# One transpose of the identity in front of each run of 256-column products that follows 512-column ones

## The chip, the cores and the metric

The kernel runs on one core of one Trainium2 chip. The metric is the device time of one execution in microseconds (us); the profile comes from one profiled execution, whose own time is given beside its span. TensorE is called PE below, its weight loads PEld; VectorE is DVE, ScalarE is ACT, GpSimd is POOL, SyncE is SP.

## The reference, cut to what matters

Two transformer blocks run one after the other on 256 positions of width 2048, all in float32.

```python
def first_block(x, mem, ...):
    mem_h = rms_norm(mem, mem_norm_g)
    x = x + hybrid_mixer(rms_norm(x, mix_norm_g), w_in, ...)          # pooling and a gated delta rule
    x = x + memory_cross_attention(rms_norm(x, xa_norm_g), mem_h, w_xq, w_xkv, w_xo)
    x = x + conv_glu_ffn(rms_norm(x, ffn_norm_g), w_gate, w_up, conv_w, conv_b, w_down)   # 2048 -> 5632 -> 2048
    return rms_norm(x, final_norm_g)

def second_block(x, c, ...):
    ...                                                                # six vectors from silu(c) @ w_ada
    x = x + gate_m * rms_norm_2(o, post_norm_mix)                      # o: two attentions and w_o
    h = modulate(rms_norm_2(x, pre_norm_ffn), shift_f, scale_f)
    f = jnp.square(jax.nn.relu(h @ w_up)) @ w_down                     # 2048 -> 8192 -> 2048
    x = x + gate_f * rms_norm_2(f, post_norm_ffn)
    return x
```

Nearly all the arithmetic is in the large products with a weight matrix: w_in, w_xkv, w_xq, w_xo, w_mix_out, w_gate, w_up, w_down and their namesakes of the second block.

## The kernel before, in words

A float32 product is made of three products of tiles of the type `F32R`: every weight tile w is split into a high part `wh` and the rest `wl`, every activation tile into `h` and `lo`, and h·wh, h·wl and lo·wh are summed in PSUM. The weights are walked in *groups* of 512 output columns (class `Group`, a few of 256), and a group in *units* of 512 KB: a DMA on SP's queue brings a unit into `w32` (`load_to`, seven units ahead), ACT writes `wh` (L216), DVE subtracts and writes `wl` (L218), and PE uses both.

There are two routines for a group. `lin_a` gives the result with the positions on the partitions: the activation is the stationary operand and 512 columns of the weight stream past it (L300, L301, L302; 256 columns in the few narrow groups). `lin_b` gives the result transposed: a block of 128 weight columns is the stationary operand and the 256 positions stream past it (L318, L319, L320). These are called *long* and *short* products below. A short group has 16 blocks of rows, each with four blocks of columns and three products, 192 products in all; a long group over 16 blocks of rows has 96, over 8 blocks 48, four such groups in a row 192.

`lin_b` makes the pooled, convolved, key and query columns, and the gate and up columns of both feed-forward parts; `lin_a` makes what must have the positions on the partitions: z, the values, and all products that go back into the residual. So the two kinds alternate: in the first feed-forward part two slabs of gate and up (768 short products), then one w_down slab (192 long ones); in the second, 384 short and 192 long ones, eight times.

The program is written in order; there is no scheduler. After each unit `pump` advances the tasks that run beside the products: attention, the delta rule, evacuations, and `ada`, which multiplies silu(c) into w_ada on DVE and turns each finished sum with four transposes on PE (L1179). Such small PE work therefore stands between the products of two units, in line on PE's queue. A transpose is a matmul with the 128x128 identity `ident` of the constant tile `cst` as the streamed operand, float32, 128 columns.

Accumulators are PSUM tiles `acc0` to `acc3`, two for each group; small work uses four other banks, `m0` to `m3`.

Of the kernel before, what the change touches and what calls it, by code (L numbers as in the profile page):

```python
# [15 lines left out]
P = 128  # L16
# [65 lines left out]
class Group:  # L82
    def __init__(self, w, segs, k0=0, nkb=KB):
        self.w, self.segs, self.k0, self.nkb = w, segs, k0, nkb
        self.n = sum(b - a for a, b in segs)
        self.calm = False
        step = 1024 // self.n
        self.units = [(self, kb, step) for kb in range(0, nkb, step)]


class Prog:
# [3 lines left out]
    def __init__(self, ctx, tc, i, o, dbg=None):  # L95
        self.tc, self.nc, self.i, self.o, self.dbg = tc, tc.nc, i, o, dbg
        self.pool = ctx.enter_context(tc.tile_pool(name="s", bufs=1))
        self.wpool = ctx.enter_context(tc.tile_pool(name="w", bufs=3))
        self.w32pool = ctx.enter_context(tc.tile_pool(name="w32", bufs=4))
        self.psum = ctx.enter_context(tc.tile_pool(name="ps", bufs=1, space=bass.MemoryType.PSUM))  # L100
        ctx.enter_context(tc.manual_schedule())
        self.seq = 0
        self.tasks = []
        self.evacs = []
        self.free_banks = ["m0", "m1", "m2", "m3"]
        self.acc_next = 0
        self.named = {}
        self.small = {}
        self.blocked = False
        self.relief = set()  # L110
        self.busy = set()
        self.rr = None
# [174 lines left out]
    def lin_a(self, g, xh, xl, evac, ready=None, eager=False):  # L287
        mm = self.nc.tensor.matmul
        n = g.n
        accs = [a[:, :n] for a in self.group_start()]  # L290
        for _, kb0, nk in g.units:
            self.check_ready(ready, kb0)
            wh, wl = self.take(g)
            for k in range(nk):
                kb = kb0 + k
                for tb in range(2):
                    ps = accs[tb]
                    h = xh(kb)[:, tb * P:(tb + 1) * P]
                    lo = xl(kb)[:, tb * P:(tb + 1) * P]
                    mm(ps, h, wh[:, k, :], start=kb == 0, stop=False)  # L300
                    mm(ps, h, wl[:, k, :], start=False, stop=False)  # L301
                    mm(ps, lo, wh[:, k, :], start=False, stop=kb == g.nkb - 1)  # L302
            self.pump()
        return self.finish_group(evac(accs), eager)

    def lin_b(self, g, xh, xl, evac, ready=None):
        mm = self.nc.tensor.matmul
        accs = self.group_start()
        for _, kb0, nk in g.units:
            self.check_ready(ready, kb0)  # L310
            wh, wl = self.take(g)
            for k in range(nk):
                kb = kb0 + k
                h, lo = xh(kb), xl(kb)
                for b in range(4):
                    ps = accs[b // 2][:, (b % 2) * T:(b % 2 + 1) * T]
                    wb, wb2 = wh[:, k, b * P:(b + 1) * P], wl[:, k, b * P:(b + 1) * P]
                    mm(ps, wb, h, start=kb == 0 and b % 2 == 0, stop=False, skip_group_check=True)  # L318
                    mm(ps, wb, lo, start=False, stop=False, skip_group_check=True)  # L319
                    mm(ps, wb2, h, start=False, stop=kb == g.nkb - 1, skip_group_check=True)  # L320
            self.pump()
        return self.finish_group(evac([a.rearrange("p (b t) -> p b t", b=2) for a in accs]))
# [1672 lines left out]
```

## Time and profile before

| | us |
|---|---|
| median of 3 runs | 2728.62 (2727.25 to 2729.43) |
| profiled execution, its own time | 2727.51 |
| its span | 2725.7 |
| PE busy | 2681.1 (98%) |
| PE weight loads busy | 2480.4 (91%) |
| DVE busy | 1854.2 (68%) |
| ACT busy | 1302.8 (48%) |
| POOL busy | 255.5 (9%) |
| mean granted clock of PE | 0.995 of full speed |

The profiled execution's time is 1.1 us below the median, and its span 1.8 us below its time. Matmuls are pipelined, so PE's busy times overlap one another: a short product "lasts" 280 ns in the rows, but the next one starts after some 115 ns. The pace, which is what a stretch costs, is therefore read as the length of a stretch divided by the products in it, and the count of weight loads (PEld) is the better count: one for each product, and hardly any that reach over the edge of the stretch.

### The profile page before, as it was taken

To read this page: it belongs to the slowest core of one execution; us is meant where nothing else is said; L and a number is where in the kernel's file an instruction comes from. 1 tells how busy PE (TensorE), PEld (TensorE's weight loads), DVE (VectorE), ACT (ScalarE), POOL (GpSimd) and SP (SyncE) were. 2 spreads that over 40 slices of the span, in tenths; PEclk is the share of its full clock that TensorE was granted. 3 is DMA by queue.
4 is the path that set the end of the run, shared out by engine and by line. 5 is a ranking of instruction groups with operands and counts; after the bars stand their busy time and mean duration, and the time that the engine had idled before them with its cause. 6 is when DMAs were issued, how large, how long until landed. Compare 5 with 4: busy or idle time off the path is not lost.

```text
span 2725.7 us, 45971 instructions
## 1 busy us (share of the span) xinstructions
PE 2681.1 (98%) x18466; PEld 2480.4 (91%) x18466; DVE 1854.2 (68%) x2331; ACT 1302.8 (48%) x1924; POOL 255.5 (9%) x229
## 2 busy tenths in 40 slices
PE   8999999999999999999999999999989999999998
PEld 8999998889989999999999888997889988999897
DVE  6665745677687778787778586677675556655555
ACT  6544533554445455354544564444554444444443
POOL 0230211000000021010100001001011000000020
PEclk9999999999999999999999999999999999999999
DMA  8644644688788888888887656544557767766654
GB/s 290 201 126 130 191 121 140 216 295 272 228 270 266 272 259 272 275 265 283 271 270 263 210 164 178 147 146 128 173 181 235 236 218 241 232 190 193 189 186 151
DMA packets 293126, 584.33 MB, mean 214 GB/s; under 512 B 21920, under 2 KB 36384, under 8 KB 292912
## 3 DMA queue, kind: packets, MB, share of 16 engines
q1 hardware_dynamic: 288528, 568.41, 65.6%
q0 software_dynamic: 3664, 11.67, 1.4%
q8 instruction: 145, 2.38, 0.4%
q10 hardware_dynamic: 720, 1.31, 0.1%
q14 instruction: 69, 0.57, 0.1%
HBM read 579.21 MB, written 2.10 MB: 213 GB/s over the span
## 4 chain that ended last, share of the span: by engine, by line
PE 93%; DVE 3%; ACT 2%; issue 1%; POOL 0%; DMA 0%; SPq 0%; DVEq 0%; POOLq 0%; ACTq 0%
PE acc L318 16%; PE acc L319 16%; PE acc L320 16%; PE acc L300 12%; PE acc L301 12%; PE acc L302 12%; DVE wl L218 1%; ACT wh L216 1%; PE m L998 1%; PE m L1051 1%; PE m L1058 1%; PE m L1148 1%; PE m L1117 1%; PE m L1001 0%; PE m L1179 0%
## 5 line engine op out<-in xcount | busy, mean ns | idle before, releaser
L218 DVE TENSOR_TENSOR wl<-w,wh 128x1024 fp32r<-128x1024 f32 x880 | 1097.1, 1249 | 805.2 <-ACT wh L216 802.8
L216 ACT ACTIVATE wh<-w 128x1024 fp32r<-128x1024 f32 x880 | 927.9, 1058 | 1121.4 <-PE acc L319 614.3
L318 PE MATMUL acc<-A,wh 128*128 128x256 f32 x3968 | 1124.1, 283 | 9.3 <-ACT A L406 7.8
L319 PE MATMUL acc<-A,wh 128*128 128x256 f32 x3968 | 1112.6, 280 | 0.7 <-DVE A L1430 0.7
L320 PE MATMUL acc<-A,wl 128*128 128x256 f32 x3968 | 1112.0, 280 | 0.8 <-DVE wl L218 0.8
L318 PEld LDWEIGHTS acc<-A,wh 128*128 128x128 f32 x3968 | 750.6, 189 | 11.4 <-ACT A L406 7.8
L320 PEld LDWEIGHTS acc<-A,wl 128*128 128x128 f32 x3968 | 756.7, 191 | 1.0 <-DVE wl L218 1.0
L319 PEld LDWEIGHTS acc<-A,wh 128*128 128x128 f32 x3968 | 749.2, 189 | 2.6 <-DVE A L1430 1.2
L300 PE MATMUL acc<-wh,A 128*128 128x512 f32 (+1 forms) x1584 | 616.0, 389 | 0.3 <-DVE r L1264 0.3
L301 PE MATMUL acc<-wl,A 128*128 128x512 f32 (+1 forms) x1584 | 608.3, 384 | 1.2 <-DVE wl L218 1.2
L302 PE MATMUL acc<-wh,A 128*128 128x512 f32 (+1 forms) x1584 | 607.8, 384 | 0.0
L301 PEld LDWEIGHTS acc<-wl,A 128*128 128x128 f32 x1584 | 298.1, 188 | 60.5 <-DVE wl L218 4.5
L302 PEld LDWEIGHTS acc<-wh,A 128*128 128x128 f32 x1584 | 297.8, 188 | 59.3
L300 PEld LDWEIGHTS acc<-wh,A 128*128 128x128 f32 x1584 | 298.0, 188 | 57.2 <-issue 0.9
L1200 DVE SCALAR_TENSOR_TENSOR r<-r,c_silu_c,r 128x1024 f32<-128x1024 f32 x128 | 170.1, 1329 | 0.0
L1200 DVE SCALAR_TENSOR_TENSOR s<-s,c_silu_c,s 128x512 f32<-128x512 f32 x128 | 95.8, 748 | 15.7 <-DMA s<-w_ada 14.4
L1886 POOL TENSOR_TENSOR s<-s 128x512 f32<-128x512 f32 x32 | 50.9, 1592 | 581.5 <-ACT s L1885 581.5
L1255 POOL TENSOR_TENSOR r<-r,rr 128x1024 f32<-128x1024 f32 x11 | 27.9, 2536 | 570.3 <-ACT r L1254 527.5
L1730 ACT ACTIVATE s<-s,c_am 128x128 f32<-128x128 f32 (+1 forms) x48 | 21.5, 448 | 92.0 <-DVE c_am L1728 92.0
L1618 POOL TENSOR_TENSOR r<-r,s 128x512 f32<-128x512 f32 x15 | 25.6, 1704 | 263.7 <-DVE s L1615 263.7
L1251 DVE SCALAR_TENSOR_TENSOR r<-r,prm,r 128x254 f32<-128x254 f32 x88 | 42.4, 481 | 1.6
L378 ACT ACTIVATE dd<-X 128x512 bf16<-128x512 f32 (+1 forms) x42 | 25.5, 606 | 21.4 <-DVE X L441 15.6
(375 smaller groups left out, 1611.8 us busy)
## 6 DMA issues: line engine op xcount, KB each, us to landing
w<-w_up SPq DMA_DIRECT2D x216, 512.0 KB, 3.8
w<-w_down SPq DMA_DIRECT2D x216, 512.0 KB, 3.9
w<-w_in SPq DMA_DIRECT2D x152, 512.0 KB, 3.7
r<-w_ada SPq DMA_DIRECT2D x128, 512.0 KB, 5.2
w<-w_gate SPq DMA_DIRECT2D x88, 512.0 KB, 4.3
w<-w_xkv SPq DMA_DIRECT2D x64, 512.0 KB, 3.9
s<-w_ada SPq DMA_DIRECT2D x128, 256.0 KB, 5.1
w<-w_mix_out SPq DMA_DIRECT2D x32, 512.0 KB, 3.7
```

The source lines that it names most:

```text
L216: nc.scalar.activation(hi[:, :m], src[:, :m], AF.Copy)
L218: eng.tensor_tensor(lo[:, :m], src[:, :m], hi[:, :m].bitcast(F32), op=OP.subtract)
L300: mm(ps, h, wh[:, k, :], start=kb == 0, stop=False)
L301: mm(ps, h, wl[:, k, :], start=False, stop=False)
L302: mm(ps, lo, wh[:, k, :], start=False, stop=kb == g.nkb - 1)
L318: mm(ps, wb, h, start=kb == 0 and b % 2 == 0, stop=False, skip_group_check=True)
L319: mm(ps, wb, lo, start=False, stop=False, skip_group_check=True)
L320: mm(ps, wb2, h, start=False, stop=kb == g.nkb - 1, skip_group_check=True)
L1200: nc.vector.scalar_tensor_tensor(acc, tiles.pop(n), self.silu_c[:, kb:kb + 1], acc, op0=OP.mult, op1=OP.add)
L1251: nc.vector.scalar_tensor_tensor(cv[:, b, s:], st[:, b, :T - s], w[k], cv[:, b, s:], op0=OP.mult, op1=OP.add)
L1255: nc.gpsimd.tensor_tensor(cv, cv, self.rr[:, None, :].to_broadcast([P, 4, T]), op=OP.mult)
L1886: nc.gpsimd.tensor_tensor(y, y, y, op=OP.mult)
```

## The change

Every run of short products that comes after long ones gets one transpose of the identity by itself in front of its first product. It writes the first 128 columns of the group's first accumulator, which the group's first product then starts anew (`start`), so no result depends on it. A flag `narrow` says whether long products have run since: `lin_a` clears it, `settle` sets it.

```diff
@@ class Prog, __init__
+        self.narrow = True
@@ lin_a
         accs = [a[:, :n] for a in self.group_start()]
+        self.narrow = False
         for _, kb0, nk in g.units:
@@
+    def settle(self, ps):
+
+        self.narrow = True
+        for r in range(1):
+            self.nc.tensor.transpose(ps[:, r * P:(r + 1) * P], self.c("ident"), self.c("ident"))
+
     def lin_b(self, g, xh, xl, evac, ready=None):
         mm = self.nc.tensor.matmul
         accs = self.group_start()
         for _, kb0, nk in g.units:
             self.check_ready(ready, kb0)
             wh, wl = self.take(g)
+            if not self.narrow:
+                self.settle(accs[0])
             for k in range(nk):
```

The program gains 17 transposes on PE and nothing on any other engine. Line numbers behind it grow by ten. On PE's queue, where the third down slab of the first feed-forward part ends and the gate columns of the next slabs begin, stood before (`acc_737` is the last accumulator of the down group, `acc_744` the first of the gate group):

```order
L301 MATMUL acc_737_11542<-wl_11566,A_629_8934 128x512
L302 MATMUL acc_737_11542<-wh_11565,A_630_8935 128x512
L318 MATMUL acc_744_11629<-A_540_7873,wh_11584 128x256 [waits Activation_49]
L319 MATMUL acc_744_11629<-A_542_7875,wh_11584 128x256
L320 MATMUL acc_744_11629<-A_540_7873,wl_11585 128x256 [waits DVE_49]
```

and stands now, with the transpose as L312:

```order
L303 MATMUL acc_737_11546<-wl_11570,A_629_8937 128x512
L304 MATMUL acc_737_11546<-wh_11569,A_630_8938 128x512
L312 MATMUL acc_744_11633<-cst 128x128
L328 MATMUL acc_744_11633<-A_540_7875,wh_11588 128x256 [waits Activation_49]
L329 MATMUL acc_744_11633<-A_542_7877,wh_11588 128x256
L330 MATMUL acc_744_11633<-A_540_7875,wl_11589 128x256 [waits DVE_49]
```

The transpose stands between the last long product and the first short one and waits for nothing; what the short products wait for is as it was. Thirteen of the 17 stand so, straight behind long products. The other four have small PE work in front of them. One is the first run of the first feed-forward part, where four transposes of `ada` stand there already; now:

```order
L1189 MATMUL m_588_8315<-cst,s_546_7899 128x128 [waits DMASW0_49,DVE_49,PE_49]
L1189 MATMUL m_588_8315<-cst,s_546_7899 128x128 x3
L312 MATMUL acc_591_8322<-cst 128x128
L328 MATMUL acc_591_8322<-A_540_7875,wh_8271 128x256 [waits Activation_49]
L329 MATMUL acc_591_8322<-A_542_7877,wh_8271 128x256
```

Here the new transpose is the fifth in a row.

## Rows read from the trace of the kernel before

**Rows 1.** The page: engines' busy time, and the chain that ended last.

```profile
PE 2681.1 (98%) x18466; PEld 2480.4 (91%) x18466; DVE 1854.2 (68%) x2331; ACT 1302.8 (48%) x1924; POOL 255.5 (9%) x229
...
PE 93%; DVE 3%; ACT 2%; issue 1%; POOL 0%; DMA 0%; SPq 0%; DVEq 0%; POOLq 0%; ACTq 0%
PE acc L318 16%; PE acc L319 16%; PE acc L320 16%; PE acc L300 12%; PE acc L301 12%; PE acc L302 12%; DVE wl L218 1%; ACT wh L216 1%; PE m L998 1%; PE m L1051 1%; PE m L1058 1%; PE m L1148 1%; PE m L1117 1%; PE m L1001 0%; PE m L1179 0%
```

**Rows 2.** The page's groups: line, shape, count, busy us, mean ns, idle before.

```profile
L318 PE MATMUL acc<-A,wh 128*128 128x256 f32 x3968 | 1124.1, 283 | 9.3 <-ACT A L406 7.8
...
L300 PE MATMUL acc<-wh,A 128*128 128x512 f32 (+1 forms) x1584 | 616.0, 389 | 0.3 <-DVE r L1264 0.3
```

**Rows 3.** Windows: length, busy (xcount) by engine, clock, DMA; short stretches behind long products.

```profile
612.87:641.13 28.26, 28.26 (x241) 28.26 (x240) 22.04 (x25) 11.76 (x12) 0.00 (x0) 1.00 0.90 308
986.36:1076.82 90.46, 90.46 (x770) 90.45 (x768) 72.66 (x71) 42.02 (x46) 9.41 (x6) 1.00 0.84 272
...
2579.09:2624.32 45.23, 45.23 (x386) 45.23 (x385) 22.09 (x21) 18.98 (x20) 3.19 (x2) 1.00 0.63 188
sum 463.58, PE 463.58 PEld 463.55 DVE 307.61 ACT 199.88 POOL 29.26; mean PE 42.14 PEld 42.14 DVE 27.96 ACT 18.17 POOL 2.66
```

**Rows 4.** Windows: short stretches behind groups of transposes.

```profile
1192.71:1211.85 19.14, 19.14 (x172) 19.14 (x170) 15.19 (x18) 11.43 (x20) 2.41 (x2) 1.00 0.74 233
1295.66:1344.72 49.06, 49.06 (x435) 49.06 (x434) 37.37 (x39) 25.24 (x34) 4.90 (x3) 1.00 0.80 262
1400.27:1476.53 76.26, 76.26 (x676) 76.26 (x674) 61.79 (x64) 38.06 (x48) 5.90 (x2) 1.00 0.83 272
2411.35:2446.81 35.46, 35.46 (x316) 35.46 (x314) 17.13 (x15) 16.91 (x25) 3.20 (x2) 1.00 0.63 193
870.00:960.00 90.00, 90.00 (x766) 90.00 (x766) 71.62 (x74) 42.30 (x47) 4.84 (x2) 1.00 0.85 280
2017.00:2088.00 71.00, 71.00 (x605) 71.00 (x604) 42.52 (x42) 34.02 (x40) 9.54 (x6) 1.00 0.76 246
```

**Rows 5.** Timeline of PE (start us, us): a short run straight behind long products.

```profile
986.14 0.39 PE L302 MATMUL acc<-wh,A 128*128 128x512 f32 x1
986.36 0.28 PE L318 MATMUL acc<-A,wh 128*128 128x256 f32 x1
986.48 0.28 PE L319 MATMUL acc<-A,wh 128*128 128x256 f32 x1
```

**Rows 6.** Timeline of PE: four transposes between short products.

```profile
1292.01 0.28 PE L320 MATMUL acc<-A,wl 128*128 128x256 f32 x1
1292.13 0.60 PE L1179 MATMUL m<-cst,r 128*128 128x128 f32 x4
1292.49 0.37 PE L318 MATMUL acc<-A,wh 128*128 128x256 f32 x1
1292.69 0.28 PE L319 MATMUL acc<-A,wh 128*128 128x256 f32 x1
```

**Rows 7.** Timeline of PE: four transposes between long and short products.

```profile
823.87 0.39 PE L302 MATMUL acc<-wh,A 128*128 128x512 f32 x1
824.10 0.60 PE L1179 MATMUL m<-cst,s 128*128 128x128 f32 x4
824.45 0.36 PE L318 MATMUL acc<-A,wh 128*128 128x256 f32 x1
824.65 0.28 PE L319 MATMUL acc<-A,wh 128*128 128x256 f32 x1
```

**Rows 8.** Timeline of PE: three transposes behind long products, further on.

```profile
1791.00 0.49 PE L1744 MATMUL m<-cst,s 128*128 128x128 f32 x3
1791.24 0.36 PE L318 MATMUL acc<-A,wh 128*128 128x256 f32 x1
```

**Rows 9.** Timeline of PE: four transposes between short products, in front of 870.

```profile
863.61 0.60 PE L1179 MATMUL m<-cst,s 128*128 128x128 f32 x4
863.97 0.36 PE L318 MATMUL acc<-A,wh 128*128 128x256 f32 x1
```

## The prediction

> **What bounds the kernel now.** I read the page's busy line first, then the chain that ended last, then the groups of PE, then windows cut exactly to single runs of products, and the timeline at their edges. PE is busy 98% of the span and holds 93% of the chain [rows 1]. Within it the short products (L318 to L320) hold 48% of the chain and the long ones (L300 to L302) 36% [rows 1]; in front of L318 PE sat idle for only 9.3 us of the whole span, 7.8 of them in one wait for ACT [rows 2]. So no other engine's edge matters here: the time is the number of products times the pace at which PE takes them.
>
> The pace of short products is the point. A window cut to one run gives it as length over weight loads. Straight behind long products the run of 768 from 986.36 takes 90.45 to 90.46 us, which is 117.8 ns for one; the eleven such stretches that are long enough to read take 463.58 us together [rows 3], at the same pace 3936 products. The same instructions on tiles of the same shape, at the same granted clock of 1.00, go faster in the four stretches of rows 4 that begin behind a group of transposes: with two loads at the edge taken off each, 168, 432, 672 and 312 products take 19.14, 49.06, 76.26 and 35.46 us, which is 113.6 ns with the slow first product (0.20 us instead of 0.12 [rows 6, 5]) and 113.4 without it. Neither pace drifts within a run: 840 products keep the slower one through 870 to 960, and 672 the faster one through 1400 to 1476 [rows 4]. Two paces, 4.4 ns apart, which a run takes on at its start and keeps: I read that as two ways in which weight loads and products can interlock, between which only an interruption moves PE. The rows don't show what the interlock is.
>
> Behind that sentence stands the Trainium skill, TensorE: Matmul & The Clock Gate, section Back-to-back issue gap: it gives the gap of warm products as a function of their columns alone, N/2.4 + 2.5, an estimate of 109.2 ns for 256 columns. The trace disagrees, with 117.8 and 113.4 ns for one shape, and it decides.
>
> **The change part by part.** It removes nothing and moves nothing but PE's rows by one. It adds 17 transposes. Thirteen stand straight behind long products, four behind small PE work.
>
> What one costs. Rows 7 show four transposes in that very place: from the start of the last long product (823.87) to that of the second short one (824.65) is 0.78 us, against 0.34 us with nothing between (986.14 to 986.48 [rows 5]). That is 0.44 us for four and 0.11 us for one. Rows 6 give the same: 1292.01 to 1292.69 is 0.68 us where two gaps of 0.12 stood, so 0.44 for four. Seventeen cost 17 x 0.11 = 1.9 us, all of it on PE and so on the chain. From below the cost is not under zero, as nothing is taken out for it; from above 0.24 us, if a lone one pays what rows 8 show for three (1791.00 to 1791.24), which would make 4.1 us. I take 1.9, from the row of the same place. The transpose reads only the constant tile, and its accumulator is the one that the next product needs in any case, so no other engine waits longer for it; in one of the 17 places a wait for ACT passes from the product to the transpose, which changes nothing.
>
> What it may give back. If a run that now begins slow begins fast, each product saves 117.8 - 113.4 = 4.4 ns. The eleven stretches of rows 3 hold 3936 products: 17.5 us. Of these 3.4 us stand in the run of 768 at 986.36 and 8.5 in five runs of 384 in the second feed-forward part, of which that at 2579.09 is the last [rows 3]. A stretch ends where the next small PE work interrupts it; behind the groups of `ada` the runs are fast already, and I count nothing there. Nor do I count the runs of the keys, of the second mixer and behind 870 and 2017, where other small work comes soon after the transpose and settles the pace anew.
>
> Whether the saving arrives. What hides behind PE must keep up with a pace 4% higher. The fast stretches themselves show that it does: through 1400.27 to 1476.53 PE is busy for all 76.26 us, with DVE at 61.79 (81%) and DMA at 0.83 [rows 4], in the same code with the same loads. In the slow stretches DVE stands at 72.66 of 90.46 (80%) and DMA at 0.84, and in the second feed-forward part below that [rows 3]; raised by 4% they come to 84% and 0.87. The highest DMA share, 0.90 at 612.87 [rows 3], would be 0.94, on a run worth 1.1 us. If that cover failed there, only that 1.1 us would go.
>
> Does one transpose make a run fast? The trace of before has no run behind a single one, so the effect is bounded from both sides. The nearest rows are groups of four. Between short products in the slow pace, on the same pair of activation tiles as these runs, there are eleven such groups without a wait in them; ten are followed by the fast pace (1292.13 is one [rows 6]), one is not (863.61 [rows 9], the stretch of 870 in rows 4). The sign shows in the first product behind the group: 0.37 us where the fast pace follows, 0.36 where it does not [rows 6, 9]. Groups of four that meet the fast pace leave it fast in seven of eight cases. Against it: directly behind long products three and four transposes stand once each, and both times the first product is 0.36 and the run slow [rows 7, 8]. And groups of eight rarely help. So a transpose can shift the interlock, but by how much depends on what stands in front of it and on how many there are. From below, the gain is zero; from above, all 17.5 us. I take the upper end, by the larger count of rows. Since ten of the thirteen direct places are the same step (a steady stream of long products, one transpose without a wait, short products), they should go together, nearly all or nearly none, and the middle is less likely than either end.
>
> The sum against the profiled execution: 2727.5 - 17.5 + 1.9 = 2711.9 us. Its time lies 1.1 us below the median of the runs shown (2728.6), so I forecast a median of 2713.0 us.
>
> **The rivals.**
>
> *One transpose doesn't move the interlock.* Then the runs keep 117.8 ns and the change is its own cost: 2728.6 + 1.9 = 2730.5 us. For it speak rows 7 and 8, the only transposes behind long products; against it ten of eleven in the place of rows 6. By the skill's rule of a gap that depends on columns alone, cited above, this is the only outcome there is.
>
> *It moves it at some places only.* The 17 places differ in what was loaded last and in how the long products ended. If about half of the gain comes: 2728.6 - 8.7 + 1.9 = 2721.8 us. For it: one of eleven groups of four failed without a visible reason [rows 9]. Against: the ten like places.
>
> *It spoils the runs that are fast now.* The four fast stretches of rows 4 are fast because the first of two groups of `ada`'s four transposes meets the slow pace in a state from which it can leave it. If a run starts in another slow state, that group may fail as the one at 863.61 did, and 168 + 432 + 672 + 312 = 1584 products fall back by 4.4 ns, 7.0 us: 2728.6 + 7.0 + 1.9 = 2737.5 us. It decides where the transpose changes the run's state and yet leaves it slow. For it: rows 9. Against: the group worked ten times of eleven.
>
> *More than forecast.* If the runs behind 864 (840 products) and 2015 (648) turn fast too, because all of PE's later steps are shifted, 1488 x 4.4 = 6.5 us more go: 2706.5 us. I leave this inside the first case's range.
>
> **How the numbers follow.** I give the first case 0.52, no effect 0.27, some places only 0.10, the loss 0.11. The first case's own range is 2706 to 2718. A measurement of this kernel can tell about 0.2%, 5.5 us, from no change. Faster by more than that: the first case and most of the third, 0.60. Within it: no effect and the rest of the partial case, 0.29. Slower: the loss, 0.11; a cost of the transposes alone cannot reach it, since even 4.1 us stays within. The range that should hold 8 in 10 reaches from 2706, the first case with its extra, to 2732, no effect with part of the upper cost; what is left out is most of the loss and a little at the fast end.
>
> **What would show it.** Right: the windows of the runs that now start at 612.87, 986.36 and 2579.09 come out at 113.4 ns a product, that of 768 near 87 us instead of 90.5; the first product behind the new transpose is 0.37 us; PE stays busy throughout. The step on the cost is wrong if the way from the last long product to the second short one is not near 0.45 us. The step on the cover is wrong if the runs are fast and a wait for DVE's `wl` appears in front of L330. The forecast is wrong if the first product is 0.36 us and the window stays at 117.8, or if the stretches of rows 4 lose their pace.

## The result and the profile after

| | us |
|---|---|
| changed kernel, median of 4 runs | 2713.23 (2708.57, 2712.86, 2713.59, 2713.91) |
| kernel before, median of 4 runs | 2727.93 (2726.39 to 2729.43) |
| ratio, with its 95% interval | 0.9948 [0.9937, 0.996] |
| profiled execution of the changed kernel | 2708.57, span 2706.8, clock 0.996 |

The change makes the kernel 0.5% faster. The profiled execution is the fastest of the four; what can make up its 5 us is shown with experiment e5. One profiled execution of the experiments below, that of e9, ran at a granted clock of 0.63 and took 3949.51 us; it is left out of e9's median.

The page of the changed kernel answers to [rows 1, 2] with the busy line and the groups of the first and the third short product; behind the bar stand busy us and mean ns of one, then the idle time in front of them:

```profile
PE 2664.7 (98%) x18483; PEld 2463.8 (91%) x18483; DVE 1853.9 (68%) x2331; ACT 1303.6 (48%) x1924; POOL 257.7 (10%) x229
...
L328 PE MATMUL acc<-A,wh 128*128 128x256 f32 x3968 | 1118.6, 282 | 9.0 <-ACT A L416 7.5
...
L330 PE MATMUL acc<-A,wl 128*128 128x256 f32 x3968 | 1105.3, 279 | 0.8 <-DVE wl L219 0.8
```

The other engines' times are as before to some 2 us; PE has 17 more instructions and is 16.4 us less busy. No wait for `wl` has appeared: 0.8 us in all stand in front of L330.

The windows of the changed kernel (length; busy and count of PE, PEld, DVE, ACT and POOL; clock, DMA share, GB/s), cut to single runs as in [rows 3, 4]; the sum is that of the eleven stretches of rows 3, the last four rows are others:

```profile
611.66:638.96 27.30, 27.30 (x243) 27.30 (x241) 20.90 (x24) 11.79 (x12) 0.00 (x0) 1.00 0.91 313
979.25:1066.39 87.14, 87.14 (x770) 87.14 (x769) 72.24 (x71) 42.07 (x46) 10.02 (x6) 1.00 0.84 282
...
1242.68:1279.52 36.84, 36.84 (x315) 36.84 (x313) 27.39 (x29) 15.27 (x16) 0.00 (x0) 1.00 0.83 284
...
2120.43:2164.05 43.62, 43.62 (x386) 43.62 (x385) 25.58 (x23) 19.99 (x22) 3.19 (x2) 1.00 0.74 242
...
2560.07:2605.38 45.31, 45.31 (x386) 45.31 (x385) 22.09 (x21) 18.96 (x20) 3.19 (x2) 1.00 0.61 187
sum 451.96, PE 451.96 PEld 451.96 DVE 305.20 ACT 200.19 POOL 30.89; mean PE 41.09 PEld 41.09 DVE 27.75 ACT 18.20 POOL 2.81
...
860.56:955.87 95.31, 95.31 (x844) 95.31 (x842) 78.97 (x83) 49.13 (x60) 7.15 (x3) 1.00 0.84 290
...
1387.49:1463.75 76.26, 76.26 (x675) 76.26 (x674) 61.78 (x64) 38.05 (x48) 5.90 (x2) 1.00 0.81 273
2392.18:2427.64 35.46, 35.46 (x315) 35.46 (x314) 17.14 (x15) 16.91 (x25) 3.19 (x2) 1.00 0.63 192
2003.00:2074.00 71.00, 71.00 (x605) 71.00 (x604) 42.12 (x40) 33.44 (x39) 9.56 (x6) 1.00 0.75 244
```

The run of 768 takes 87.14 us instead of 90.46, which is the fast pace; that of 384 at 2120 takes 43.62 instead of 45.22. But 312 products from 1242.68 (36.84 us) and 384 from 2560.07 (45.31) keep 117.8 ns, and so does a second run of 384, at 2471. Together the eleven stretches went from 463.58 to 451.96 us, 11.6 us less and not 17.5: 2856 of the 3936 products turned, 12.6 us at 4.4 ns, and the slow first products behind the transposes (0.20 us instead of 0.12) take 0.9 back. Something that was not counted came on top: the 840 products behind the groups of `ada` take 95.31 us here. Before they took 99.02:

```profile
863.97:962.99 99.02, 99.02 (x844) 99.02 (x842) 77.80 (x82) 49.17 (x60) 7.28 (x3) 1.00 0.85 280
```

The stretches that were fast stay so to a hundredth, and the 648 behind 2003 stay slow.

The timeline of PE in the changed kernel (start, us) shows three new transposes, L312, at their places; each first short product behind one is the one that gives the sign:

```profile
978.99 0.40 PE L304 MATMUL acc<-wh,A 128*128 128x512 f32 x1
979.22 0.27 PE L312 MATMUL acc<-cst 128*128 128x128 f32 x1
979.25 0.37 PE L328 MATMUL acc<-A,wh 128*128 128x256 f32 x1
979.45 0.28 PE L329 MATMUL acc<-A,wh 128*128 128x256 f32 x1
...
1242.42 0.40 PE L304 MATMUL acc<-wh,A 128*128 128x512 f32 x1
1242.65 0.27 PE L312 MATMUL acc<-cst 128*128 128x128 f32 x1
1242.68 0.36 PE L328 MATMUL acc<-A,wh 128*128 128x256 f32 x1
1242.88 0.28 PE L329 MATMUL acc<-A,wh 128*128 128x256 f32 x1
...
821.93 0.60 PE L1189 MATMUL m<-cst,s 128*128 128x128 f32 x4
822.37 0.27 PE L312 MATMUL acc<-cst 128*128 128x128 f32 x1
822.39 0.36 PE L328 MATMUL acc<-A,wh 128*128 128x256 f32 x1
```

From the last long product to the second short one it is 0.46 us (978.99 to 979.45) against 0.34 without the transpose [rows 5]: 0.12 us for one. To the hundredth the steps at 979, where the run turned fast, and at 1242, where it did not, are the same; only the first product differs, 0.37 against 0.36 us.

### The profile page after: what moved, and what is told of

It is laid out like the page before. It is cut to its first block, busy times and chain, and to the rows that moved or that the text cites. A ratio compares the mean times of both kernels' runs of the same rounds, so it can differ in the third digit from the quotient of the medians.

```text
span 2706.8 us, 46004 instructions
## 1 busy us (share of the span) xinstructions
PE 2664.7 (98%) x18483; PEld 2463.8 (91%) x18483; DVE 1853.9 (68%) x2331; ACT 1303.6 (48%) x1924; POOL 257.7 (10%) x229
## 4 chain that ended last, share of the span: by engine, by line
PE 93%; DVE 3%; ACT 2%; issue 1%; POOL 0%; DMA 0%; POOLq 0%; DVEq 0%; ACTq 0%
PE acc L328 16%; PE acc L329 16%; PE acc L330 16%; PE acc L302 12%; PE acc L303 12%; PE acc L304 12%; DVE wl L219 1%; ACT wh L217 1%; PE m L1008 1%; PE m L1061 1%; PE m L1068 1%; PE m L1158 1%; PE m L1127 1%; PE m L1011 0%; PE m L1189 0%
## 5 line engine op out<-in xcount | busy, mean ns | idle before, releaser
L330 PE MATMUL acc<-A,wl 128*128 128x256 f32 x3968 | 1105.3, 279 | 0.8 <-DVE wl L219 0.8
L330 PEld LDWEIGHTS acc<-A,wl 128*128 128x128 f32 x3968 | 750.7, 189 | 1.0 <-DVE wl L219 1.0
```

## The experiments

All runs, with the kernel before of the same session beside each:

| run | what it is | median us (runs) | before | ratio [95%] |
|---|---|---|---|---|
| e1_two | two transposes | 2723.62 (11) | 2726.48 | 0.9986 [0.9977, 0.9995] |
| e2_three | three | 2723.69 (11) | 2726.48 | 0.9990 [0.9981, 0.9999] |
| e3_product | a short product instead | 2728.42 (11) | 2726.48 | 1.0004 [0.9993, 1.0015] |
| e4_no_third | without the third of the 17 | 2715.14 (5) | 2726.48 | 0.9957 [0.9944, 0.9969] |
| e5_again | the change | 2712.42 (5) | 2727.56 | 0.9946 [0.9934, 0.9959] |
| e6_mixed | two or four at four places | 2715.41 (5) | 2727.56 | 0.9957 [0.9945, 0.997] |
| e7_half | a transpose of a 64 x 128 piece | 2724.35 (11) | 2727.56 | 0.9987 [0.9978, 0.9996] |
| e8_second | in front of the second group | 2717.60 (5) | 2727.56 | 0.9963 [0.9950, 0.9975] |
| e9_sixth | behind six short products | 2704.48 (5) | 2723.17 | 0.9929 [0.9916, 0.9943] |
| e10_sixth_two | the same, two | 2711.07 (5) | 2723.17 | 0.9952 [0.9939, 0.9964] |
| e11_again | the change | 2714.57 (6) | 2723.17 | 0.9970 [0.9959, 0.9982] |
| e12_sixth | e9 once more | 2705.82 (5) | 2727.31 | 0.9924 [0.9910, 0.9938] |

And what the windows of their profiles, cut as above, say of the eleven stretches of rows 3 (F 113.3 ns, S 117.8 ns). The expectations speak of ten like places; with the 240, which they leave out, it is eleven.

| products | before, e3 | one: after, e4, e5, e11 | two: e1 | three: e2 | half: e7 | behind six: e10, e12 |
|---|---|---|---|---|---|---|
| 240 | S | F | S | S | F | F |
| 768 | S | F | S | S | S | F |
| 576 | S | F | S | S | S | F |
| 312 | S | S | F | F | F | F |
| 72 | S | F | S | S | F | F |
| 384, first | S | F, F, S, F | S | F | F | F |
| 384, second | S | F | S | S | S | F |
| 384, third | S | F | F | F | F | F |
| 48 | S | F | S | S | F | F |
| 384, fourth | S | S | F | F | F | F |
| 384, fifth | S | S | S | S | F | F |

**e1, two transposes.**

```diff
-        for r in range(1):
+        for r in range(2):
```

> Two transposes instead of one in front of each run of short products that follows long ones. Theory (landing): a run's pace is decided by the few nanoseconds at which its first product lands; long and short products keep one beat, a transpose does not. One transpose lands near the border, so that seven of ten like places took the fast pace in the profiled execution and three (312, 384 and 384 products, 1080 together) did not. A second transpose moves every landing by the same amount, to where seven of the nine other groups of transposes of that trace were followed by the fast pace: all ten places fast, 1080 x 4.4 ns = 4.8 us less, 17 x 0.11 = 1.9 us more, 2713.2 - 2.9 = 2710.3 us. Rival (chance): any break gives each place a new draw at seven in ten; about three of the ten stay slow, others than before, and only the cost is added: 2715.1 us. Rival (toggle): a second transpose undoes the first, all ten slow: 2727.9 + 3.8 = 2731.7 us.

All three were wrong in their way. The windows of e1 (columns as above), the runs of 768, 312 and 648:

```profile
987.78:1078.32 90.54, 90.54 (x772) 90.54 (x770) 71.66 (x71) 42.02 (x46) 10.20 (x6) 1.00 0.83 272
1257.28:1292.74 35.46, 35.46 (x315) 35.46 (x314) 27.30 (x28) 15.29 (x16) 0.00 (x0) 1.00 0.88 291
2015.83:2089.37 73.54, 73.54 (x651) 73.54 (x650) 46.20 (x48) 36.21 (x43) 9.57 (x6) 1.00 0.80 256
```

Nearly the opposite of one transpose: 768 slow again, 312 fast, and 648 fast too. Of the eleven, 1080 products are fast. They and the 648 give 1728 x 4.4 = 7.6 us, and 34 transposes at 0.12 cost 4.1: 3.5 us, as the ratio says (0.14% of 2726 is 3.8). More of the same interruption is not better.

**e2, three transposes.** The same line with `range(3)`.

> Three transposes in each place. Theory (landing): where three land is not shown by a place of this kind; the landing worked out from one and two lies beside the border again, so the ten places go together in the main, fast or slow: fast 2713.2 - 4.8 + 3.8 = 2712.2 us, slow 2727.9 + 5.7 = 2733.6 us; the three transposes of another tile behind long products in the trace before (first product 0.36 us, run slow) speak for slow. Rival (chance): seven of ten fast as with one: 2713.2 + 3.8 = 2717.0 us.

They did not go together: 1464 of 3936 products fast. Of the landing, what held is that the number matters; what I had worked out of where they land did not.

**e3, a product in place of the transpose.**

```diff
...
-            self.nc.tensor.transpose(ps[:, r * P:(r + 1) * P], self.c("ident"), self.c("ident"))
+        self.nc.tensor.matmul(ps[:, :T], wb, h, start=True, stop=True, skip_group_check=True)
...
```

> The transpose is replaced by one more short product of the same shape (128 weight columns, 256 positions, the operands of the run's first product), which the run's first product then overwrites. Theory (landing): a product of the kind that keeps the beat shifts nothing, so the runs stay at 117.8 ns and the time is that of the kernel before and 17 more products: 2727.9 + 17 x 0.12 = 2729.9 us. Rival (any extra instruction in front of the run, or the restart of the accumulator, breaks the slow pace): as with the transpose, 2713.2 us.

The theory held. The same run of 768 in e3:

```profile
986.41:1076.86 90.45, 90.45 (x770) 90.45 (x769) 72.71 (x71) 42.02 (x46) 9.22 (x6) 1.00 0.84 272
```

90.45 us, as before, and all eleven stretches slow. An instruction more in front of the run, or an accumulator started twice, does nothing there, if it is one of the run's own kind.

**e4, without the third transpose.**

```diff
...
+        self.runs += 1
-        for r in range(1):
+        for r in range(self.runs != 3):
```

> The change without one of its 17 transposes, the third: the one that stands as fifth behind four transposes of ada, in front of the 24, 120, 168 and 840 short products that ran slow before and fast after. Theory: this one transpose made all four of these runs fast, since a run that is fast stays fast over the groups of four between them; without it they go back: 0.10 + 0.51 + 0.74 + 3.71 = 5.1 us more, 0.1 less, 2718.2 us, and the 768 behind them stay fast. Rival: they are fast because all that PE does is shifted from the first two transposes on, and stay fast: 2713.1 us.

Neither was right. The 120 and 168 were slow, as the theory had it, but the 24 and the 840 were fast without that transpose; the 840 are the first row, the 768 the second:

```profile
864.66:959.96 95.30, 95.30 (x843) 95.30 (x842) 76.80 (x80) 49.15 (x60) 7.15 (x3) 1.00 0.86 284
983.33:1070.47 87.14, 87.14 (x771) 87.14 (x769) 72.24 (x71) 42.06 (x46) 10.02 (x6) 1.00 0.84 281
```

**e5 and e11, the changed kernel again.** No edit.

> The changed kernel once more. Theory (the landing is set by what stands directly in front): the ten like places come out as in the first profile of it, 240, 768, 576, 72, 48 and three times 384 products fast, 312, 384 and 384 slow, as they did in the run without the third transpose; what differs between executions (2708.6 us in the first profile, 2713 to 2714 in the others) is the stretch of 840 behind the groups of ada, 3.7 us, and short stretches of the first stage. Median about 13 us below the kernel before. Rival (chance): the seven fast places are others this time.

> The changed kernel on the same chip, to compare with the two: about 14 us below the kernel before; 240, 768, 576, 72, 48 and 384 products at the second and third place of the second feed-forward part fast, 312, 384 and 384 slow, as in the three profiles of this kernel and its near copies so far; 840 and the first 384 either way.

In e5 the runs of 840, 768, the first and the fourth 384:

```profile
863.61:962.63 99.02, 99.02 (x844) 99.02 (x842) 76.90 (x80) 49.18 (x60) 7.25 (x3) 1.00 0.82 276
986.07:1073.21 87.14, 87.14 (x771) 87.14 (x770) 72.25 (x71) 42.06 (x46) 10.04 (x6) 1.00 0.83 281
2129.06:2174.37 45.31, 45.31 (x387) 45.31 (x386) 25.69 (x23) 19.94 (x22) 3.19 (x2) 1.00 0.73 233
2481.47:2526.78 45.31, 45.31 (x387) 45.31 (x385) 22.01 (x20) 18.96 (x20) 3.18 (x2) 1.00 0.63 188
```

Ten of the eleven stretches give one answer in all four profiles with a single whole transpose (table): it is no draw, against the rival of chance. Only the first 384, the place that follows the second mixer, was slow in one. e11's paces came out as expected; its time did not: 8.6 us below the kernel before, which was itself faster in that session, instead of some 14. The 840 were fast in the first profile and in e11 and slow in e5; the 120 and 168 in front of them fast in the first alone. So the 840, 120 and 168, and with them 5.0 us, are no firm part of the change. The executions differ by such stretches: the profiled one of e5 took 2718.91 us against 2708.57 of the first, 10.3 us more, and nine stretches with 2472 products that are fast in the first (264 and 168 at the start, 120, 168, 840, 408 behind 1560, 48, 72, and the first 384) are slow in it: 2472 x 4.4 = 10.9 us.

**e6, other numbers at four places.**

```diff
...
+        self.runs += 1
-        for r in range(1):
+        for r in range({6: 2, 11: 2, 16: 2, 17: 4}.get(self.runs, 1)):
```

> One transpose in 13 places as in the change, two at the three places whose run (312, 72 and then 648, 384 products) was slow behind one and fast behind two, four at the last place (384 products), which was slow behind one, two and three. Theory (the landing is set by what stands directly in front): the places keep the answer that they gave for this number, so 312 + 648 + 384 = 1344 products turn fast, 6.0 us, less six more transposes, 0.7 us: 5.3 us below the changed kernel of the same call; the last place is open, 1.7 us either way. Rival (history): a changed place changes every landing behind it, and the sum is a draw: between 3 us faster and 5 us slower than the changed kernel.

The theory fell at all three edited places for which it had forecast an answer, and the time, 3.0 us above e5's, is one that the rival allowed. The runs of 312 and of the fourth 384 in e6, each behind two transposes:

```profile
1251.04:1287.88 36.84, 36.84 (x316) 36.84 (x315) 27.39 (x29) 15.26 (x16) 0.00 (x0) 1.00 0.85 285
2482.91:2528.22 45.31, 45.31 (x387) 45.31 (x386) 22.00 (x20) 18.96 (x20) 3.19 (x2) 1.00 0.64 187
```

Both are slow, 648 and the fifth 384 too, while in e1 two transposes made 312, 648 and the fourth 384 fast. The unedited places gave e5's answers. What differs is what ran earlier: the 576 ahead of the 312 were slow in e1 and fast in e6. So a place's answer seems to hang on what PE did before the long products too; no run here shows how.

**e7, a shorter transpose.**

```diff
-            self.nc.tensor.transpose(ps[:, r * P:(r + 1) * P], self.c("ident"), self.c("ident"))
+            self.nc.tensor.transpose(ps[:, :64], self.c("ident")[:64], self.c("ident")[:64, :64])
```

> One transpose in each place, of a 64 x 128 piece of the identity, so that 64 columns stream instead of 128. Theory (landing): it shifts the first product by another amount, so other places are fast: of the ten like places at least two change sides against one whole transpose, and of the total gain nothing can be said beforehand: between the kernel before and the changed one, or beyond it. Rival (that one transpose stands there counts, not its length): the same places fast and slow as with one, and 17 x 0.05 us less for the shorter transposes: 1 us below the changed kernel.

Six of the eleven change sides, as the theory of landing had it: 768, 576 and the second 384 slow, 312, the fourth and the fifth 384 fast. The runs of 768 and of the fifth 384 in e7:

```profile
983.63:1074.19 90.56, 90.56 (x769) 90.56 (x769) 71.64 (x71) 41.90 (x46) 9.85 (x6) 1.00 0.82 272
2570.26:2613.90 43.64, 43.64 (x386) 43.64 (x386) 22.09 (x21) 18.91 (x20) 3.20 (x2) 1.00 0.65 194
```

The rival's saving of 1 us was wrong as well: the small transpose costs more. It also has 64 rows instead of 128, so the length alone is not what was changed. The timeline of PE in e7:

```profile
983.11 0.39 PE L304 MATMUL acc<-wh,A 128*128 128x512 f32 x1
983.43 0.27 PE L312 MATMUL acc<-cst 64*128 64x64 f32 x1
983.63 0.39 PE L328 MATMUL acc<-A,wh 128*128 128x256 f32 x1
983.86 0.28 PE L329 MATMUL acc<-A,wh 128*128 128x256 f32 x1
```

From the last long to the second short product 0.75 us stand against 0.46 for the whole one: 0.41 us for one, some 7 us for 17.

**e8, in front of the second group.** The transpose goes behind 192 short products instead of in front of the first.

```diff
...
-            if not self.narrow:
+            if i == 0 and self.groups == 2:
                 self.settle(accs[0])
```

> The transpose moved from the front of a run to the front of its second group, that is behind 192 short products. Theory (a run holds its pace until PE is interrupted, and one transpose can move it): the first 192 products of these runs stay at 117.8 ns, and the pace changes at the transpose, in most places to 113.3; the products behind it in the slow stretches are 120, 576, 384, 120, 216 and five times 192, 2376 together: 10.5 us if all turn, and 1.9 us of cost, 8.6 us below the kernel before. Rival (the pace is set at the start, behind the long products, and a single transpose between short ones moves nothing): 1.9 us above the kernel before.

The theory held as to the pace, and the time is 10.1 us less where 8.6 were expected. That sum has other parts than forecast, though: 216 of its products were fast before already, 768 turned slow, and 576 behind 2017 and the 840, which it left out, were fast. The windows of e8: the first 384 products on both sides of their transpose, then 96 and 576 on both sides of another:

```profile
2126.89:2149.50 22.61, 22.61 (x193) 22.61 (x192) 12.41 (x11) 9.45 (x10) 0.00 (x0) 1.00 0.75 236
2149.53:2171.40 21.87, 21.87 (x196) 21.87 (x194) 13.16 (x13) 10.51 (x12) 3.19 (x2) 1.00 0.72 240
...
1393.51:1404.49 10.98, 10.98 (x99) 10.98 (x98) 6.10 (x5) 5.33 (x12) 0.00 (x0) 1.00 0.66 195
...
1404.52:1472.44 67.92, 67.92 (x579) 67.92 (x578) 56.12 (x59) 32.65 (x36) 4.91 (x2) 1.00 0.82 277
```

And the timeline at the first of them:

```profile
2149.38 0.28 PE L330 MATMUL acc<-A,wl 128*128 128x256 f32 x1
2149.50 0.27 PE L311 MATMUL acc<-cst 128*128 128x128 f32 x1
2149.53 0.36 PE L328 MATMUL acc<-A,wh 128*128 128x256 f32 x1
2149.73 0.28 PE L329 MATMUL acc<-A,wh 128*128 128x256 f32 x1
```

The first 192 products take 22.61 us (117.8 ns each), the next 192 take 21.87 (113.4 behind a slow first), one transpose between them and nothing else. All eleven transposes of e8 that stood directly behind 48 or more short products in the slow pace, in the first block's cross attention and the two feed-forward parts, were followed by the fast one. It works the other way too: 96 products behind a group of `ada` take 10.98 us, the fast pace, and the 576 behind the transpose 67.92 us, 117.8 ns each; of three that met the fast pace, two turned it slow. The first product is 0.36 us at 2149.53, though its run is fast.

Not every instruction of another kind does it. In two places of each profile, at some 83 and 843 us, four products of `dd` with a constant block (float32, 128 columns as in a transpose, but no transpose) stand between short products without a wait. In the trace before:

```profile
843.38 0.60 PE L361 MATMUL m<-dd,cst 128*128 128x128 f32 x4
843.74 0.36 PE L318 MATMUL acc<-A,wh 128*128 128x256 f32 x1
```

The 120 products before them and the 168 behind them both take 117.8 ns. In the 13 profiles at full clock such a group met the slow pace 19 times and the fast one seven times, and the pace behind it was the same each time. A single one of them was not tried.

**e9 and e12, behind the first six short products.** Each of the eleven runs starts slow straight behind long products [rows 3], and the transpose works on short products in the slow pace. So it goes behind the first six, where the run's second accumulator is not yet in use; in the runs behind 822 and 1983 it goes in front of the second group, and four places lose theirs: 13 in all.

```diff
...
+        late = first and self.runs not in (1, 3, 8, 9, 10, 11)
+        early = self.groups == 2 and self.runs in (3, 11)
...
                 for b in range(4):
+                    if late and i == k == 0 and b == 2:
+                        self.settle(accs[1])
```

> The transpose stands behind the first six short products of a run that follows long ones directly (11 places: in front of the first product into the run's second accumulator), so that it meets short products in the slow pace, as all transposes of the run before did that changed the pace; in the runs behind 822 and 1983 it stands in front of the second group, as there; the other four places have none. Theory (a transpose meets steady slow products always at the same point of their beat, and long ones not): all ten like places turn fast but for their first six products, with the stretches behind the two others: 234 + 762 + 570 + 306 + 66 + 42 + 5 x 378 + 120 + 576 = 4566 products, 20.3 us, and 840 behind the fast 120, 3.7 us; less 13 transposes, at most 0.3 us each between short products (their slow first product counted): 4 us. 20 us below the kernel before, some 6 us below the changed kernel. Rival (as behind long products, some places take it and some don't): two or three of the ten stay slow, no faster than the changed kernel.

> The kernel with the transpose behind the first six short products once more, for a profile at the full clock. Theory (between short products in the slow pace a transpose always works, behind long ones only in some places): the stretches of 234, 762, 570, 306, 66, 42 and five times 378 products all at 113.3 ns, each behind six at 117.8; 576 behind 1983 fast too; 840 fast if the 120 and 168 in front of it are. About 18 to 20 us below the kernel before, as in its first timing (2705.0 against 2723.2 us). Rival: two or three of these stretches slow, and the time of the first timing comes from elsewhere.

e12 repeats e9, whose profiled execution is the one left out above, and has the profile. The runs of 768 and of the fifth 384 behind their first six, and the 840:

```profile
982.69:1069.16 86.47, 86.47 (x765) 86.47 (x764) 72.23 (x71) 41.54 (x46) 9.27 (x6) 1.00 0.85 283
2559.65:2602.60 42.95, 42.95 (x382) 42.95 (x380) 22.10 (x21) 18.47 (x20) 3.20 (x2) 1.00 0.65 196
863.31:958.61 95.30, 95.30 (x844) 95.30 (x842) 78.27 (x82) 49.12 (x60) 7.15 (x3) 1.00 0.85 290
```

All eleven are fast, with 120, 576 and 840 beside them. Expected from the pace: 5406 products x 4.4 ns = 23.8 us, less 13 x 0.12 = 1.6, is 22.2; measured 0.76%, 20.7 us [16.9, 24.5]. In the session with e11 this version takes 2704.48 us, the kernel before 2723.17 and the change 2714.57: 18.7 and 10.1 us less, for 20 and 6 expected.

**e10, two behind the six.** The same with `range(2)`.

> The same with two transposes in each of the 13 places. Theory (the landing decides): the second transpose moves the first product behind it by the same amount in all places, to where, in the records of the runs so far, a group of transposes was followed by the slow pace each time (the last transpose 3.7 to 4.4 ns behind the beat of 6.67 ns): the ten like places all stay slow, and the time is 1 to 5 us above the kernel before. Rival (a break is a break, two are at least as good as one): as with one, and 13 x 0.11 = 1.4 us above it.

The theory's landing failed again: the eleven and the 576 are fast, as with one. Two transposes made three of the eleven fast behind long products (e1) and all eleven here, so behind slow short products the second does no harm to the pace. Its median is 6.6 us above e9's: 13 more transposes are 1.6 of them, and 3.7 would be the 840, which are slow in its profile and fast in that of e12.

## Why the prediction was right, and where it was not

The median came out at 2713.2 us for a forecast of 2713.0, and most of the mechanism held; the agreement to 0.2 us is partly luck: stretches that were not counted made up for counted ones that failed, and of the other three executions no profile shows which stretches were fast.

- *Two paces, held for a whole run, between which only an interruption moves PE*: right, and e8 shows it within one run; that the pace comes of an interlock of weight loads and products no run shows. That same-shaped products took 117.8 and 113.4 ns at a clock of 1.00 on either side of one transpose is also against the rule of the Trainium skill that the prediction cites, TensorE: Matmul & The Clock Gate, section Back-to-back issue gap, by which the gap follows from the columns alone. The prediction left out that the same section keeps that formula for a single, isolated product and says that in a stream weight loads and products set the spacing together, which fits the picture of an interlock better; it gives one spacing for a number of columns, though, not of two.
- *Cost*: 0.12 us for one instead of 0.11, 2.0 us instead of 1.9, on PE alone.
- *Gain*: 17.5 us forecast, 11.6 measured on the same eleven stretches. The step that failed is "they should go together, nearly all or nearly none": seven of the ten like places turned fast, three did not (312, 384, 384 products; 1080 x 4.4 = 4.8 us), and that in every profile. They are alike in the program's order and, at 979 and 1242, in the steps of the timeline to a hundredth, and still answered differently. The first 384 (1.7 us) is not firm either.
- *"Straight behind long products" the runs are slow*: true of the eleven, but the prediction passed over a run in the second mixer that is as long as one of them and stands straight behind 24 long products. Its 48 products from 1706.72 take 5.46 us in the trace before, 113.8 ns each, with no transpose in front, and three transposes (e2) turn it slow. So long products don't always leave the slow pace behind.

```profile
1706.72:1712.18 5.46, 5.46 (x49) 5.46 (x48) 2.45 (x2) 3.10 (x4) 0.00 (x0) 1.00 0.67 196
```

- *The uncounted stretches*: in the profiled execution the 840 and the 24, 120 and 168 in front of them turned fast, 5.1 us, which made up for the three that failed. It was the rival of more than forecast, by half (648 stayed slow), and e4, e5 and e11 show that it comes and goes.
- *The sum again*: the windows hold the slow first products, so of the 2.0 us of cost 1.1 are still to be added: 2727.5 - 11.6 - 5.1 + 1.1 = 2711.9 us against 2708.6 in the profiled execution. Of the 3.3 us left, 1.5 are one place that the change doesn't touch: behind a wait, 24 products at 1672.79 ran at a granted clock of 0.61 before, and at 1.00 now, as these two windows show, of before and of after. Another 1.2 are in front of the first stretch of rows 3, which starts at 611.66 instead of 612.87. The rest is not traced.

```profile
1672.79:1677.20 4.41, 4.41 (x27) 4.41 (x25) 3.71 (x4) 0.00 (x0) 2.32 (x1) 0.61 0.67 190
```

```profile
1659.67:1662.55 2.88, 2.88 (x28) 2.88 (x26) 2.82 (x4) 0.00 (x0) 1.99 (x1) 1.00 0.63 185
```

- *Cover*: right. In the stretch of 768, now at 113.3 ns, DVE is busy 72.24 of 87.14 us (83%, forecast 84), DMA 0.84; at 611 DMA is at 0.91 and its products still come every 113.3 ns.
- *The fast stretches of rows 4 are spoilt*: did not happen, 76.26 and 35.46 us as before. That a transpose can do so, e8 shows.
- *The sign of the first product (0.37 fast, 0.36 slow)*: no sign. It fits at 979 and 1242, but the runs behind 822 and 2149 (e8) are fast behind 0.36.
- *"I take the upper end, by the larger count of rows"*: those rows were read right as to short products (ten of eleven groups there, eleven of eleven single ones in e8), but the upper end was taken from them for a place behind long products, where rows 7 and 8 stood nearer and said slow.

Open stays what decides behind long products. It is not chance (e5, e11), not any instruction (e3), not the count alone (e6); the size of the transpose matters (e7), and it seems that what ran before the long products does (e6). My picture of a first product that lands at a point of a beat forecast e3 and, loosely, e7, and missed e1, e2, e6 and e10.

## What to carry to other kernels

Where a matmul stream of one shape shows two steady paces at the same clock, a single transpose can move it from one to the other, as here; other small matmuls need not (e8). Put it where it meets the slow stream itself, not at the seam behind another shape, and look at each place in the trace, since it can turn the better pace into the worse as well. Count places that look alike as separate draws with fixed answers, and bound the effect by rows with the same work in front. A few products given up at the slow pace bought a firm answer here: 0.7 to 0.8% instead of 0.3 to 0.5.

## What the runs showed of the hardware that was not expected

- One 128-column transpose changes the pace of the same 256-column products from 117.8 to 113.3 ns or back, and the pace then holds for as many as 768 products. One more product of their own kind in front of a run (e3), or four products of another kind between short ones (at 843.38), change nothing.
- These two paces are not the only ones: the keys of the first block's cross attention take 120.0 ns for a product of the same shape at a clock of 1.00 (8.52 us for 71 from 327.29), before and after the change.
- Behind long products the answer of a place repeats from run to run (ten of eleven places), yet in most places is turned round by a second transpose (e1) and in six by a smaller one (e7).
- The transpose of a 64 x 128 piece between full-size products costs 0.41 us (e7), the 128 x 128 one 0.12.
